# Decay blocks of an SSD branch: a preset and an accumulating transfer in place of a subtraction on VectorE

## The chip, the cores and the metric

The kernel runs on one core of one Trainium2 chip. The metric is the device time of one execution in microseconds (us), median of three runs. Lower is better.

## The reference, cut to what matters

The program is a decoder trunk of two layers on 256 tokens of width 1024. A layer is half a SwiGLU feed-forward (FFN), a token mixer, and another half FFN. The mixer runs two branches on one normalised input: a gated DeltaNet branch and a Mamba-2 state-space (SSD) branch, and merges them. The change lies in the SSD branch, which works in two chunks of 128 tokens with 32 heads in 4 groups of 8:

```python
a_cum = jnp.cumsum(log_a, axis=2)
seg = a_cum[:, :, :, None] - a_cum[:, :, None, :]
decay = jnp.where(causal, jnp.exp(jnp.where(causal, seg, 0.0)), 0.0)
cb = jnp.einsum("bclgn,bcsgn->bclsg", Cc, Bc)
y_diag = jnp.einsum("bclsg,bclsgh,bcsghp->bclghp", cb, decay, xdt)
```

For each group, chunk and head the kernel needs the 128 by 128 block cb times exp(a_cum[l] - a_cum[s]), zero where l is before s.

## The kernel before, in words

TensorE does all large products in three passes of split operands: a weight tile wraw (128 x 1024) comes in by a transfer from SP's queue, ScalarE rounds it to a high part whi, VectorE forms the low part wlo = wraw - whi, and TensorE multiplies. There are five buffers each for wraw, whi and wlo (`NRAW`, `NSPL`), so weights are prepared up to five tiles ahead. These two splits are the bulk of the work of ScalarE and VectorE throughout.

Inside a mixer the work is a list of named steps, `ORDER`. The tail of it is what concerns us: `... R R P R g100 g101 D0 S0 x10 T0 D1 x11 g110 g111 S1 x20 T1 o x21 N D2 y S2 D3 x30 x31 T2 ...`. R is a step of the DeltaNet recurrence; P forms the masked products cb of the SSD branch; g are gate products; x10 and x11 are the two units that make the inputs xs of group 1; D*g* makes the decay block of group *g*, S*g* and T*g* are the two halves of its SSD step; o and N are the branch product of DeltaNet, y the first transposes for that of the SSD branch. The list gives a priority. The framework's scheduler then sets the order in which instructions stand on each engine, and at run time each engine works strictly in that order; an instruction that waits holds all behind it on its engine.

Names that the text uses, with their lines:

- dc (L1060): the decay block of a group, 128 x 2048 floats, partition s, and along the row head, chunk and l. It lives in slot sA for groups 0 and 2 and sB for 1 and 3; those slots belong to kP and qP of the recurrence until the products ksb and qsb (L954) of its last step have read them, and dc2 takes dc0's slot once ydb (L1115) has read it, dc3 that of dc1.
- In `decay` (L1059): a transfer from SP's queue (L1061) broadcasts eight rows of a_cum, written to DRAM earlier (rdram), to all 128 partitions; VectorE subtracts the partition's own a_cum (ac), broadcast along the row; VectorE clamps at 0 from above (L1071, recorded as L78); ScalarE takes the exponential (L1072, recorded as L68); VectorE multiplies with the masked cb, cbm (L1073, recorded as L71).
- cbb (L1045, L1046): the four products of P, in PSUM banks of a rotating set of four. The fourth needs the bank that vb <- ob, os (L998), the last output of the recurrence, reads on VectorE. cbt holds the masked products.
- `ssd(g)` (L1087): xsb transposes of xsT, VectorE forms xD, xdt and xe, TensorE multiplies ydb = dc x xdt and yob, VectorE adds up into yz, ScalarE squares it (jk), the sums are sss, GpSimd takes the power -0.5 (srr, L210), ScalarE scales yz with it.
- `conv` (L625): ca on ScalarE, three steps on VectorE (ca, L74), then xsT by a SiLU on ScalarE. The exponential and the SiLU need different function tables, so an ACT_TABLE_LOAD stands between them.
- `dn_T` (L1150): transposes oT, og on VectorE, its high part bh on ScalarE, its low part bl on VectorE; these are the stationary operands of the branch product b (L335 to L337). `ss_T` makes the transposes yT for the SSD branch.

Two helpers record most lines: every ScalarE operation has L68, every two-operand VectorE operation L71. GpSimd otherwise does small powers and the accumulating transfers of the FFN (wsum at L156, h at L460).

Of the kernel before, what the change touches and what calls it, by code (L numbers as in the profile page):

```python
# [10 lines left out]
AF = mybir.ActivationFunctionType  # L11
ALU = mybir.AluOpType
# [4 lines left out]
P = 128  # L17
# [36 lines left out]
def trunk_kernel(ctx, tc, x, wst, wsm, norms, lpar, rpar, cst, out):  # L54
    nc = tc.nc
    V, A, G, PE = nc.vector, nc.scalar, nc.gpsimd, nc.tensor
# [10 lines left out]
    def act(o, i, func=AF.Copy, **kw):  # L67
        return A.activation(out=o, in_=i, func=func, **kw)  # L68

    def tt(o, a, b, op):  # L70
        return V.tensor_tensor(out=o, in0=a, in1=b, op=op)  # L71
# [4 lines left out]
    def ts(o, a, s1, op0, sc2=None, op1=None):  # L76
        if op1 is None:
            return V.tensor_scalar(out=o, in0=a, scalar1=s1, scalar2=None, op0=op0)  # L78
        return V.tensor_scalar(out=o, in0=a, scalar1=s1, scalar2=sc2, op0=op0, op1=op1)
# [7 lines left out]
    def trb(name):  # L87
        return trp.tile([P, 512], F32, tag="tr", name=name)
# [4 lines left out]
    def small(shape, name, bufs=2):  # L93
        return sm.tile(shape, F32, tag=name, name=name, bufs=bufs)
# [124 lines left out]
    h = cpool.tile([P, 2, D], F32, name="h")  # L219
# [373 lines left out]
    def mixer(l, nxt):  # L593
# [51 lines left out]
        ac = small([P, 2, 40], "ac", 1)  # L645
# [3 lines left out]
        rdram = dram.tile([40, S], F32, tag="rdram", name="rdram")  # L649
# [376 lines left out]
        late = {}  # L1026
# [11 lines left out]
        def ssd_pre():  # L1038
            BT, CT = late["BC"][:, 0:4], late["BC"][:, 4:8]
            cbt = slots.tile([P, 3 * GS, P], F32, tag="sF", name="cbt")  # L1040
            late["cbx"] = cbx = cbt[:, 2 * GS :]
            late["cbm"] = cbm = cbt[:, : 2 * GS].rearrange("p (g t) l -> p g t l", g=GS)
            for g in range(GS):
                cbb = trb("cbb")
                PE.matmul(cbb[:, 0 : 2 * P], BT[:, g, 0:P], CT[:, g, :], start=True, stop=True)  # L1045
                PE.matmul(cbb[:, 2 * P : 3 * P], BT[:, g, P : 2 * P], CT[:, g, P : 2 * P], start=True, stop=True)  # L1046
                tt(
                    cbm[:, g],
                    cbb[:].rearrange("p (t o l) -> p t o l", t=2, o=2)[:, :, 0, :],
                    U[:, None, :].to_broadcast([P, 2, P]),  # L1050
                    ALU.mult,
                )
                act(cbx[:, g], cbb[:, P : 2 * P])
            yield

        xsT = {}
# [1 line left out]

        def decay(g):  # L1059
            dc = slots.tile([P, 8, 2, P], F32, tag=("sA", "sB")[g % 2], name="dc")  # L1060
            nc.sync.dma_start(  # L1061
                dc[:].rearrange("p h t l -> p (h t l)"),
                rdram[8 * g : 8 * g + 8].rearrange("a b -> (a b)").partition_broadcast(P),
            )
            tt(
                dc[:], dc[:],
                ac[:, :, 8 * g : 8 * g + 8].rearrange("p t h -> p h t")[:, :, :, None].to_broadcast([P, 8, 2, P]),
                ALU.subtract,
            )
            dv = dc[:].rearrange("p h t l -> p (h t l)")  # L1070
            ts(dv, dv, 0.0, ALU.min)  # L1071
            act(dv, dv, AF.Exp)  # L1072
            tt(dc[:], dc[:], late["cbm"][:, g, None].to_broadcast([P, 8, 2, P]), ALU.mult)  # L1073
            decs[g] = dc

# [133 lines left out]
        def step(name):  # L1209
# [10 lines left out]
            elif kind == "M":  # L1220
                masks()
            elif kind == "I":
                next(inv, None)
            elif kind == "R":
                next(rc, None)
            elif kind == "b":
                bcm(*num)
            elif kind == "d":
                zdm(*num)
            elif kind == "x":  # L1230
                xs_unit(*num)
            elif kind == "P":
                drain(ssd_pre())
            elif kind == "D":
                decay(*num)
            elif kind == "g":
                gate(*num)
            elif kind == "S":
                heads[num[0]] = ssd(*num)
                next(heads[num[0]])  # L1240
            elif kind == "T":
                drain(heads[num[0]])
            elif kind == "o":
                dn_T(0)
            elif kind == "y":
                ss_T(0)
            elif kind == "N":
                dn_branch()
# [190 lines left out]
```

## Time and profile before

| | us |
|---|---|
| median of three runs (1543.25 to 1544.58) | 1544.3 |
| span of the profiled execution, first to last instruction | 1539.7 |
| between the two | 4.6 |
| TensorE busy | 1522.8 |
| VectorE busy | 1229.7 |
| ScalarE busy | 944.8 |
| GpSimd busy | 81.8 |

The granted clock is 0.999. Engines: PE is TensorE's matmuls and PEld its weight loads, DVE is VectorE, ACT is ScalarE, POOL is GpSimd, SP is the queue of most transfers. A row of a timeline reads: start, duration, engine, line, operation, output <- inputs, shapes, and in brackets how long the engine stood idle before and who ended that. A row of waits reads: who waited, for whom, us in total, times, the longest. A row of a tile has the shortest, median and longest duration in ns. A row of DMA queues has packets, MB, and the share of all sixteen DMA engines over the span. Times count from the start of the span; layer 0's mixer makes its decay blocks between 394 and 495, layer 1's 761 us later.

### The profile page before, as it was taken

What the parts mean: (1) busy time and instruction counts of PE and PEld (TensorE: products, weight loads), DVE (VectorE), ACT (ScalarE), POOL (GpSimd) and SP (SyncE); (2) the same over time, 40 slices, a digit from 0 to 9 for tenths busy, and PEclk for the clock granted to TensorE, in tenths of its full rate; (3) what the DMA queues carried; (4) which work ended last, traced back from release to release, by engine and by line L of the source; (5) the groups of instructions that cost most, each with busy time, mean ns of one, the idle gap of its engine ahead of it and who ended that gap; (6) DMA issues with size and microseconds to landing.
All of it is one profiled execution on the core that took longest, in us unless ns stands there. A gap on an engine that the chain in (4) does not pass through costs nothing.

```text
span 1539.7 us, 29072 instructions
## 1 busy us (share of the span) xinstructions
PE 1522.8 (99%) x11473; PEld 1384.4 (90%) x11473; DVE 1229.7 (80%) x1859; ACT 944.8 (61%) x1532; POOL 81.8 (5%) x92
## 2 busy tenths in 40 slices
PE   8999999999999999999999999999999999999998
PEld 7999889999888888999899998899998888899997
DVE  6878769967899766789778887689589996677886
ACT  5655667765665645555555566676756666455565
POOL 0000110000000000000100012010000000000010
PEclk9999999999999999999999999999999999999999
DMA  7687775653565556587867687665345555556785
GB/s 277 190 265 231 226 228 167 187 164 111 178 213 171 163 166 196 185 256 211 261 225 225 208 253 229 197 193 180 117 141 202 179 170 186 176 177 195 247 241 156
DMA packets 98831, 305.73 MB, mean 199 GB/s; under 512 B 22837, under 2 KB 23813, under 8 KB 97670
## 3 DMA queue, kind: packets, MB, share of 16 engines
q1 hardware_dynamic: 93796, 290.95, 57.2%
q0 software_dynamic: 4608, 12.58, 5.1%
q8 instruction: 90, 1.47, 0.4%
q14 instruction: 47, 0.39, 0.1%
q10 hardware_dynamic: 290, 0.33, 0.1%
HBM read 297.72 MB, written 1.92 MB: 195 GB/s over the span
## 4 chain that ended last, share of the span: by engine, by line
PE 89%; DVE 4%; ACT 2%; DMA 2%; issue 1%; SPq 1%; POOL 0%; POOLq 0%; ACTq 0%; DVEq 0%
PE fc L346 10%; PE fc L340 9%; PE fc L345 9%; PE t L366 9%; PE o L337 4%; PE o L335 4%; PE o L336 4%; PE f L366 3%; PE b L335 3%; PE b L337 3%; PE b L336 3%; PE p L336 2%; PE p L337 2%; PE p L335 2%; PE xs L345 1%; PE xs L340 1%
## 5 line engine op out<-in xcount | busy, mean ns | idle before, releaser
L71 DVE TENSOR_TENSOR wlo<-wraw,whi 128x1024 fp32r<-128x1024 f32 x488 | 591.8, 1221 | 186.7 <-ACT whi L68 172.2
L68 ACT ACTIVATE whi<-wraw 128x1024 fp32r<-128x1024 f32 x488 | 511.6, 1059 | 271.0 <-PE fc L345 92.5
L346 PE MATMUL fc<-uW,wlo 128*128 128x256 f32 x1280 | 354.9, 277 | 0.0
L340 PE MATMUL fc<-uW,whi 128*128 128x256 f32 x1280 | 354.1, 277 | 0.0
L345 PE MATMUL fc<-uW,whi 128*128 128x256 f32 x1260 | 348.3, 276 | 0.0
L340 PEld LDWEIGHTS fc<-uW,whi 128*128 128x128 f32 x1280 | 240.5, 188 | 0.8
L346 PEld LDWEIGHTS fc<-uW,wlo 128*128 128x128 f32 x1280 | 240.5, 188 | 0.0
L345 PEld LDWEIGHTS fc<-uW,whi 128*128 128x128 f32 x1260 | 236.5, 188 | 0.8
L366 PE MATMUL t<-whi,uW 128*128 128x512 f32 x512 | 165.3, 397 | 0.0
L366 PEld LDWEIGHTS t<-whi,uW 128*128 128x128 f32 x512 | 95.9, 188 | 21.6 <-issue 1.3
L68 ACT ACTIVATE whi<-wsum 128x1024 fp32r<-128x1024 f32 x64 | 68.0, 1062 | 58.8 <-PE fc L345 32.9
L366 PE MATMUL t<-wlo,uW 128*128 128x512 f32 x256 | 100.2, 392 | 0.0
L71 DVE TENSOR_TENSOR wlo<-wsum,whi 128x1024 fp32r<-128x1024 f32 x64 | 78.2, 1221 | 7.9 <-ACT whi L68 5.6
L335 PE MATMUL b<-whi,bh 128*128 128x512 f32 x192 | 76.1, 398 | 0.3
L336 PE MATMUL b<-wlo,bh 128*128 128x512 f32 x192 | 74.9, 390 | 0.0
L337 PE MATMUL b<-whi,bl 128*128 128x512 f32 x192 | 74.2, 393 | 0.0
L340 PE MATMUL xs<-uW,whi 128*128 128x256 f32 x256 | 72.8, 284 | 0.0
L346 PE MATMUL xs<-uW,wlo 128*128 128x256 f32 x256 | 71.4, 279 | 0.0
L345 PE MATMUL xs<-uW,whi 128*128 128x256 f32 x254 | 70.6, 278 | 0.0
L335 PE MATMUL o<-whi,gh 128*128 128x512 f32 (+1 forms) x160 | 62.0, 388 | 0.0
L337 PE MATMUL o<-whi,gl 128*128 128x512 f32 (+1 forms) x160 | 61.8, 386 | 0.0
L336 PE MATMUL o<-wlo,gh 128*128 128x512 f32 (+1 forms) x160 | 61.7, 386 | 0.0
(337 smaller groups left out, 3291.7 us busy)
## 6 DMA issues: line engine op xcount, KB each, us to landing
wraw<-in_wst_dram SPq DMA_DIRECT2D x504, 512.0 KB, 4.9
wsum<-in_wst_dram SPq DMA_DIRECT2D x16, 512.0 KB, 7.3
wsum<-in_wst_dram POOLq DMA_DIRECT2D x16, 512.0 KB, 8.7
dc<-rdram SPq DMA_DIRECT2D x8, 1024.0 KB, 8.5
nw<-in_norms_dram SPq DMA_DIRECT2D x6, 512.0 KB, 5.9
h<-u POOLq DMA_DIRECT2D x12, 256.0 KB, 6.8
gb<-rdram SPq DMA_DIRECT2D x8, 256.0 KB, 5.6
h<-in_x_dram SPq DMA_DIRECT2D x4, 256.0 KB, 3.7
```

What stands on the lines that cost most here:

```text
L68: return A.activation(out=o, in_=i, func=func, **kw)
L71: return V.tensor_tensor(out=o, in0=a, in1=b, op=op)
L335: PE.matmul(ps, lh, rh, start=start, stop=False)
L336: PE.matmul(ps, lh, rl, start=False, stop=False)
L337: return PE.matmul(ps, ll, rh, start=False, stop=stop)
L340: PE.matmul(ps, wh, mh, start=start, stop=False)
L345: PE.matmul(ps, wh, ml, start=False, stop=False)
L346: PE.matmul(ps, wl, mh, start=False, stop=stop)
L366: ins = PE.matmul(ps[t][:], st, mv, start=k0 == 0 and j == 0, stop=k0 == KT - 2 and j == 5)
```

## The change

ScalarE first writes the negated row term into the block, -ac broadcast along the row; then GpSimd issues a transfer that adds the broadcast rows of rdram to what stands there; VectorE's subtraction is gone. Clamp, exponential and multiply stay. The exponential is queued on ScalarE behind the last read of cbb (`issue_after` sets an order on that instruction's own engine alone, so it does not hold the clamp on VectorE).

```diff
-                act(cbx[:, g], cbb[:, P : 2 * P])
+                late["read"] = act(cbx[:, g], cbb[:, P : 2 * P])
...
         def decay(g):
             dc = slots.tile([P, 8, 2, P], F32, tag=("sA", "sB")[g % 2], name="dc")
-            nc.sync.dma_start(
-                dc[:].rearrange("p h t l -> p (h t l)"),
-                rdram[8 * g : 8 * g + 8].rearrange("a b -> (a b)").partition_broadcast(P),
+            dv = dc[:].rearrange("p h t l -> p (h t l)")
+            act(
+                dc[:],
+                ac[:, :, 8 * g : 8 * g + 8].rearrange("p t h -> p h t")[:, :, :, None].to_broadcast([P, 8, 2, P]),
+                scale=-1.0,
             )
-            tt(
-                dc[:], dc[:],
-                ac[:, :, 8 * g : 8 * g + 8].rearrange("p t h -> p h t")[:, :, :, None].to_broadcast([P, 8, 2, P]),
-                ALU.subtract,
+            G.dma_start(
+                out=dv, in_=rdram[8 * g : 8 * g + 8].rearrange("a b -> (a b)").partition_broadcast(P), accum_op=ALU.add
             )
-            dv = dc[:].rearrange("p h t l -> p (h t l)")
-            ts(dv, dv, 0.0, ALU.min)
-            act(dv, dv, AF.Exp)
+            with tc.issue_after(late["read"].ins):
+                ts(dv, dv, 0.0, ALU.min)
+                act(dv, dv, AF.Exp)
             tt(dc[:], dc[:], late["cbm"][:, g, None].to_broadcast([P, 8, 2, P]), ALU.mult)
```

The scheduler answers with another order at several places; both layers get the same. On VectorE, at the end of the recurrence in layer 0, before:

```order
L71 TENSOR_TENSOR wlo<-wraw,whi 128x1024 x2
L71 TENSOR_TENSOR dc<-dc,ac 128x2048
L71 TENSOR_TENSOR vb<-ob,os 128x512
L71 TENSOR_TENSOR cbt<-cbb,cs 128x256 x2
L1004 TENSOR_REDUCE so<-o_4924 128x4
L71 TENSOR_TENSOR cbt<-cbb,cs 128x256
L74 SCALAR_TENSOR_TENSOR so<-so,oe 128x4
L71 TENSOR_TENSOR cbt<-cbb,cs 128x256
L71 TENSOR_TENSOR vb<-vb,so_2294 128x512
L78 TENSOR_SCALAR dc<-dc 128x2048
L71 TENSOR_TENSOR dc<-dc,ac 128x2048
```

At the same place now (so is the recurrence's sum of squares, the two dc are blocks 0 and 1):

```order
L71 TENSOR_TENSOR wlo<-wraw,whi 128x1024
L78 TENSOR_SCALAR dc<-dc 128x2048
L71 TENSOR_TENSOR vb<-ob,os 128x512
L71 TENSOR_TENSOR cbt<-cbb,cs 128x256 x2
L1004 TENSOR_REDUCE so<-o_4924 128x4
L71 TENSOR_TENSOR cbt<-cbb,cs 128x256
L74 SCALAR_TENSOR_TENSOR so<-so,oe 128x4
L71 TENSOR_TENSOR cbt<-cbb,cs 128x256
L71 TENSOR_TENSOR vb<-vb,so_2294 128x512
L78 TENSOR_SCALAR dc<-dc 128x2048
L71 TENSOR_TENSOR dc<-dc,cbt 128x2048
```

The clamp of block 0, which waits for its transfer, now stands where the subtraction stood, ahead of vb; the clamp of block 1 stands where the second subtraction stood. The multiply of block 1 has moved ahead of xD, xdt and xe of group 0, from behind the products ydb.

On ScalarE, between the two squares of group 0 and the last convolution of x11, before (the exponential of block 2 comes further down, behind the next unit's ca):

```order
L68 ACTIVATE jk,sss<-yz 128x512 x2
L68 ACTIVATE whi<-wraw 128x1024
L68 ACTIVATE ca<-xs,lp 128x256
L68 ACTIVATE yz<-yz,srr 128x512 x2
L68 ACTIVATE whi<-wraw 128x1024
L68 ACTIVATE xsT<-ca 128x256
L68 ACTIVATE whi<-wraw 128x1024 x2
L68 ACTIVATE xsT<-ca 128x256
L68 ACTIVATE ca<-xs,lp 128x256
```

The same place now:

```order
L68 ACTIVATE jk,sss<-yz 128x512
L68 ACTIVATE ca<-xs,lp 128x256
L68 ACTIVATE whi<-wraw 128x1024
L68 ACTIVATE xsT<-ca 128x256
L68 ACTIVATE yz<-yz,srr 128x512 x2
L68 ACTIVATE whi<-wraw 128x1024
L68 ACT_TABLE_LOAD
L68 ACTIVATE dc<-dc 128x2048
L68 ACT_TABLE_LOAD
L68 ACTIVATE xsT<-ca 128x256
L68 ACTIVATE ca<-xs,lp 128x256
```

The exponential of block 2, with a table load on each side, has moved up to directly behind the scaling of yz and ahead of the last convolution. On VectorE the clamp and the multiply of block 2 have moved up with it, ahead of that convolution's three steps, and sss of group 0 has moved back behind two weight splits.

On ScalarE, at the start of the branch product of DeltaNet, before:

```order
L68 ACTIVATE jk,sss<-yz 128x512
L68 ACTIVATE ca<-xs,lp 128x256
L68 ACTIVATE bh<-og 128x512
L68 ACTIVATE xsT<-ca 128x256
L68 ACTIVATE yz<-yz,srr 128x512 x2
```

The same place now (yz and srr are those of group 1, bh the first two operands of b):

```order
L68 ACTIVATE xsT<-ca 128x256
L68 ACTIVATE jk,sss<-yz 128x512
L68 ACTIVATE ca<-xs,lp 128x256
L68 ACTIVATE whi<-wraw 128x1024
L68 ACTIVATE yz<-yz,srr 128x512 x2
L68 ACTIVATE bh<-og 128x512 x2
```

The first bh has moved from ahead of the scaling of yz to behind it. On TensorE two transposes oT and the four transposes of the first yT have moved ahead of the first b; on GpSimd the four transfers stand between the powers so and srr.

## The prediction

> **What bounds the kernel now.** I read the page first, then the waits of TensorE, then the time windows of the mixer of layer 0 (the 400:480 stretch; layer 1 repeats it 761 us later).
>
> ```profile
> span 1539.7 us, 29072 instructions
> ...
> PE 1522.8 (99%) x11473; PEld 1384.4 (90%) x11473; DVE 1229.7 (80%) x1859; ACT 944.8 (61%) x1532; POOL 81.8 (5%) x92
> ...
> PE 89%; DVE 4%; ACT 2%; DMA 2%; issue 1%; SPq 1%; POOL 0%; POOLq 0%; ACTq 0%; DVEq 0%
> ```
>
> TensorE is busy for 99% of the span and holds 89% of the chain that ended last. Taking work off another engine pays only where TensorE stands still, and any new stop of TensorE is a loss at full size. So the next view is who makes TensorE wait, and where the other engines are nearly full:
>
> ```profile
> PE cbb L1045 <- DVE vb L71: 1.9, 2, 1.3
> PE xsb L1101 <- ACT xsT L68: 1.9, 2, 0.9
> ...
> 400.00:420.00 20.00, 19.40 (x114) 16.61 (x113) 18.40 (x20) 12.27 (x16) 1.01 (x1) 1.00 0.48 172
> 420.00:440.00 20.00, 20.00 (x174) 17.56 (x173) 19.40 (x29) 13.26 (x22) 1.61 (x1) 1.00 0.68 221
> 440.00:460.00 20.00, 18.92 (x193) 17.43 (x192) 19.90 (x29) 14.50 (x20) 1.34 (x1) 1.00 0.64 210
> ```
>
> In a window the third busy figure, after PE and PEld, is VectorE: 18.4 to 19.9 of 20 us, so it really is full where the decay blocks are made. Yet TensorE loses only 1.9 us at cbb and 1.9 us at xsb, both layers together. That sum, 3.8 us, is the most that relief of VectorE can give here: 0.25% of the time.
>
> **The change part by part.** The operations on a decay block, eight in all (four per layer, dc0 to dc3 below):
>
> ```profile
> L1061 SPq DMA_DIRECT2D dc<-rdram x8: 326/404/1490, 394.0 to 1212.5; - x8
> L71 DVE TENSOR_TENSOR dc<-dc,ac x8: 2277/2284/2292, 401.9 to 1231.4; 128x2048 f32<-128x2048 f32 x8
> L78 DVE TENSOR_SCALAR dc<-dc x8: 1216/1220/1224, 408.3 to 1248.8; 128x2048 f32<-128x2048 f32 x8
> L68 ACT ACTIVATE dc<-dc x8: 1903/1918/1924, 411.0 to 1252.3; 128x2048 f32<-128x2048 f32 x8
> ...
> DMA to landing us min/median/max: 6.2/8.5/10.6
> ```
>
> Removed: 8 subtractions of 2.28 us on VectorE, 18.3 us, of which at most the 3.8 us above can show. Added: 8 presets on ScalarE. Before has no such operation; the nearest row is the exponential of the same 128x2048 shape, 1.9 us, and I take that. 15 us more on ScalarE, itself 12 to 15 us busy in 20, are covered, except where the order puts a preset ahead of something TensorE needs. The plain transfer leaves SP's queue (its weight loads move up, worth nothing as TensorE never waits for them there) and becomes an accumulating one on GpSimd, issued only after the preset. What that one costs:
>
> ```profile
> q1 hardware_dynamic: 93796, 290.95, 57.2%
> q0 software_dynamic: 4608, 12.58, 5.1%
> ...
> wsum<-in_wst_dram POOLq DMA_DIRECT2D x16, 512.0 KB, 8.7
> ...
> L156 POOL DMA_DIRECT2D wsum<-in_wst_dram x16: 862/870/1035, 69.6 to 1485.8; - x16
> ```
>
> q0 carries the accumulating transfers. By bytes, q1 takes 57.2% / 290.95 MB x 1539.7 us = 3.0 us of all sixteen engines per MB, q0 5.1% / 12.58 x 1539.7 = 6.2 us. A block is 1.05 MB: 3.2 us plain, 6.5 us accumulating. So from issue to landing I expect the quickest plain block plus the difference, 6.2 + 3.3 = 9.5 us, as the low estimate, and the median accumulating 512 KB plus another half, 8.7 + 3.3 = 12.0, as the high one. I take 9.5: the DMA share of the 400:420 window is 0.48, the lowest of the three. Issuing holds GpSimd 0.9 us, and GpSimd is otherwise idle.
>
> The Trainium skill, DMA: Bandwidth & Descriptors, section "Anatomy of one DMA — SWDGE (gpsimd) path", fits a transfer issued from GpSimd as about 2.0 us plus its bytes at 436 GB/s; by that a block lands 4.4 us after issue, an estimate, and the first term below would be -1.9 and not +1.8. The trace does not agree for accumulating transfers: half a block takes 8.7 us.
>
> *First place: cbb, after dc0.* VectorE's order keeps vb directly behind the first operation on dc0, formerly the subtraction, now the clamp, so whoever waits for dc0 holds vb, and vb holds TensorE's fourth cbb. (GpSimd's power for so also stands behind two block issues, which are long over by then.)
>
> ```profile
> 391.29 1.09 PE L954 MATMUL ksb<-St,kP 128*64 128x128 f32 x16
> ...
> 392.25 0.55 ACT L68 ACTIVATE ca<-xs,lp 128x256 f32<-128x256 f32 x1
> ...
> 404.15 0.68 DVE L71 TENSOR_TENSOR vb<-ob,os 128x512 f32<-128x512 f32 x1
> ...
> 408.34 1.22 DVE L78 TENSOR_SCALAR dc<-dc 128x2048 f32<-128x2048 f32 x1
> ...
> 404.88 0.48 PE L1045 MATMUL cbb<-BC 128*128 128x256 f32 x1 [0.60 <-DVE vb L71]
> ...
> 1152.94 0.55 ACT L68 ACTIVATE ca<-xs,lp 128x256 f32<-128x256 f32 x1
> ...
> 1166.25 0.48 PE L1045 MATMUL cbb<-BC 128*128 128x256 f32 x1 [1.28 <-DVE vb L71]
> ```
>
> dc0's slot is free when ksb ends at 392.4; ScalarE is free at 392.8. Preset to 394.7, landing at 404.2, clamp 1.2 to 405.4, vb 0.7 to 406.1; cbb then starts 1.3 us later than its 404.88. In layer 1 the same steps from 1153.5 give 1155.4, 1164.9, 1166.8: 0.5 us later than 1166.25. Together +1.8. Were the landing at 6.2, both old waits would vanish (0.6 and 1.28: -1.9); at 12.0 it is +6.8.
>
> *dc1* follows in the same queue: 404.2 + 6.5 = 410.7 at the earliest, some 413 with weight loads between. VectorE comes to its clamp 3.5 us after vb's end (the old 404.8 to 408.34), at 409.6, and stops for 1 to 3.5 us, where the second subtraction stood with 2.3. Queued behind are dc0's multiply, weight splits and the inputs of ydb; five weight buffers cover the splits. I take 0.3 us per layer, bounds 0 and 3: +0.6.
>
> *Second place: xsb.* On ScalarE the exponential of dc2 now stands behind the scaling of yz, which waits for GpSimd's srr; and on VectorE dc2's multiply stands ahead of the last convolution of the xs unit, whose result (xsT) the last transposes of xsb need.
>
> ```profile
> 426.81 1.28 ACT L68 ACT_TABLE_LOAD   x1 [3.56 <-DVE ca L74]
> ...
> 431.29 1.61 POOL L210 TENSOR_TENSOR srr<-sss,mhalf 128x2 f32<-128x2 f32 x1 [23.59 <-DVE sss L79]
> ...
> 432.93 1.34 ACT L68 ACTIVATE yz<-yz,srr 128x512 f32<-128x512 f32 x2 [1.32 <-POOL srr L210]
> ...
> 443.56 0.47 DVE L74 SCALAR_TENSOR_TENSOR ca<-xs,lp,ca 128x253 f32<-128x253 f32 x1
> 444.12 0.42 ACT L68 ACTIVATE xsT<-ca 128x256 f32<-128x256 f32 x1 [1.26 <-DVE ca L74]
> ...
> 444.59 0.33 PE L1101 MATMUL xsb<-cs,xsT 128*128 128x128 f32 x1 [0.93 <-ACT xsT L68]
> ...
> L71 DVE TENSOR_TENSOR wlo<-wraw,whi 128x1024 fp32r<-128x1024 f32 x488 | 591.8, 1221 | 186.7 <-ACT whi L68 172.2
> L68 ACT ACTIVATE whi<-wraw 128x1024 fp32r<-128x1024 f32 x488 | 511.6, 1059 | 271.0 <-PE fc L345 92.5
> ```
>
> srr started at 431.29. Ahead of it now stand two weight splits (2.4) and three convolution steps (1.4) more, a multiply (2.3) less: +1.5, and TensorE's 1.6 us of lateness, so 434.4. Then srr 1.6, yz 1.3, whi 1.1, table 1.3, exponential 1.9, multiply 2.3, three steps 1.4, a split 1.2, xsT 0.4: 446.9. TensorE, late by 1.6, would come there at 444.59 - 0.93 + 1.6 = 445.3. It waits 1.6 us, or 2.7 where dc1's multiply, moved ahead of ydb's inputs, costs VectorE half its length; I take 2.4, which is 1.5 more than the old 0.93. Two layers: +3.0, bounds -1.9 (the wait goes, as the subtraction does) and +5.
>
> *Third place: the first b.* bh, which the branch product b needs, stood ahead of the scaling of yz on ScalarE; now it stands behind it.
>
> ```profile
> 458.41 0.17 DVE L79 TENSOR_SCALAR sss<-sss 128x2 f32<-128x2 f32 x1
> ...
> 458.66 1.61 POOL L210 TENSOR_TENSOR srr<-sss,mhalf 128x2 f32<-128x2 f32 x1 [25.77 <-DVE sss L79]
> ...
> 458.76 0.62 ACT L68 ACTIVATE bh<-og 128x512 fp32r<-128x512 f32 x1
> ...
> 460.30 1.34 ACT L68 ACTIVATE yz<-yz,srr 128x512 f32<-128x512 f32 x2 [0.61 <-POOL srr L210]
> ...
> 451.09 0.33 SPq L1061 DMA_DIRECT2D dc<-rdram  x1
> ...
> 458.58 0.71 PE L1154 MATMUL oT<-cs,vb 128*128 128x128 f32 x5
> 459.44 0.50 PE L335 MATMUL b<-whi,bh 128*128 128x512 f32 x1
> ```
>
> With sss as early as before, yz ends at 461.6, bh at 462.2, and b starts there instead of at 459.44. Six transposes (0.14 each) move into that gap, 0.8 us, so 2.0 us is lost; sss itself comes some 0.3 later, as a step of xsT moved ahead of its square. 2.3 per layer: +4.6, bounds +1.5 and +8 for both layers. dc3's slot came free at 451.1, when SP issued the plain transfer; a preset later, 453.0, the new one is issued and lands at 462.5. VectorE comes to that clamp behind the bl that follows bh, after 462.2, so I cost it at nothing, and at 2.5 us per layer if the landing takes 12.0.
>
> Sum: 1.8 + 0.6 + 3.0 + 4.6 = +10.0 us on a span of 1539.7; the median of 1544.3 lies 4.6 above the span, and I leave that offset: 1554.3.
>
> **The rivals.** *The accumulating transfer is quick and the full VectorE decides.* Blocks land in about 6 us, VectorE is rid of 18.3 us in its fullest stretches, and the waits at cbb and xsb go: -3.8 us, and with bh's inputs ready no new one: 1540.5. For it: VectorE at 19.9 of 20. Against: q0's price per byte, and b's new place behind yz does not depend on the transfer. It decides where a block lands in under 8.6 us, from which cbb is no later than before (it is late by 0.9 us a layer at 9.5), and sss comes 2 us earlier, so that bh is ready when b is. Chance 0.07. The Trainium skill's fit above is this case.
>
> *Waits are exchanged.* cbb comes out even, the xsb gaps close (-1.9) because VectorE is lighter, b costs less than 1.5 a layer: 1542 to 1546. The gaps were made on VectorE, and a lighter one could bring sss early enough. Chance 0.20.
>
> *GpSimd cannot issue while VectorE works.* The Trainium skill, SBUF — State Buffer, section "Who interferes with whom", says a transfer issued by GpSimd starves while VectorE is in a two-port mode. The mechanism here: each of the first three issues per layer slips behind clamps and splits on a VectorE that is never idle, by one such operation, 1.2 us, and dc1's late landing reaches ydb: another 3.6 to 5 us per layer: 1561 to 1564. Sixteen issues of 862 to 1035 ns on a VectorE 80% busy speak against it: spread 0.17 us. Chance 0.13.
>
> That the change does not do what it says can be left out: the order has the presets and transfers and no subtraction.
>
> **How the numbers follow.** The forecast, the new places of exponential and bh cost more than the relief brings, +4 to +16 us, has 0.60. About 0.2%, 3.1 us, is what a measurement of this kernel can tell from no change. Slower by more: 0.60 + 0.13 = 0.73; within: 0.20; faster: 0.07. The range 1544 to 1564 leaves out the faster rival, half of the exchange case and a few hundredths above.
>
> **What would show it.** In the changed profile: presets near 1.9 us; accumulating blocks landing after 9 us or more; VectorE's wait before the first clamp ended by the DMA; TensorE's cbb wait near 2 us, its xsb wait near 2.4, and a new wait at the first b, near 2, released by ScalarE's bh. If b shows no wait, or landings are at 6 us, the steps that carry the forecast are wrong.

## The result and the profile after

The changed kernel takes 1556.7 us (median of five runs, 1553.8 to 1557.0), the kernel before 1544.0 (five runs, 1543.2 to 1544.6): a ratio of 1.0083, 95% interval 1.0072 to 1.0094, 12.7 us slower. The profiled execution was the quickest of its five, 1553.8, with a span of 1552.0, 12.3 more than the 1539.7 of before.

The page of the changed kernel, its span, busy times, the queue of GpSimd's transfers and the chain that ended last:

```profile
span 1552.0 us, 29084 instructions
...
PE 1524.9 (98%) x11473; PEld 1386.5 (89%) x11473; DVE 1213.9 (78%) x1851; ACT 959.0 (62%) x1540; POOL 87.6 (6%) x100
...
q0 software_dynamic: 5760, 20.97, 7.9%
...
PE 79%; DVE 6%; issue 6%; ACT 4%; DMA 3%; SPq 1%; POOL 1%; POOLq 0%; ACTq 0%; DVEq 0%
```

VectorE is 15.8 us less busy, and TensorE's share of the chain fell from 89% to 79%: it now waits. For whom, the waits of TensorE say:

```profile
PE cbb L1045 <- DVE vb L71: 6.3, 2, 3.3
PE b L335 <- ACT bh L68: 5.2, 2, 2.6
...
PE xsb L1101 <- ACT xsT L68: 1.9, 3, 1.0
```

Against before, cbb rose from 1.9 to 6.3, a wait at the first b is new, and xsb has the same sum. The rows of the decay blocks (shortest, median, longest in ns) and their landing:

```profile
L68 ACT ACTIVATE dc<-ac x8: 1901/1914/1935, 393.8 to 1222.6; 128x2048 f32<-128x2048 f32 x8
L1067 POOL DMA_DIRECT2D dc<-rdram x8: 867/912/931, 396.0 to 1224.8; - x8
...
  DMA dc<-rdram: 14.1, 6
...
DMA to landing us min/median/max: 9.3/10.6/14.1
```

A preset takes 1.9 us, a block lands 10.6 us after issue (8.5 before), and six of the eight clamps had to wait for that, 14.1 us in all. The two places in layer 0, VectorE's rows first, then TensorE's, ScalarE's, and TensorE's again:

```profile
406.81 1.23 DVE L78 TENSOR_SCALAR dc<-dc 128x2048 f32<-128x2048 f32 x1 [3.76 <-DMA dc<-rdram]
407.95 0.68 DVE L71 TENSOR_TENSOR vb<-ob,os 128x512 f32<-128x512 f32 x1
```

```profile
408.69 0.70 PE L1045 MATMUL cbb<-BC 128*128 128x256 f32 x2 [3.33 <-DVE vb L71]
```

```profile
465.81 1.33 ACT L68 ACTIVATE yz<-yz,srr 128x512 f32<-128x512 f32 x2 [0.54 <-POOL srr L210]
467.05 0.61 ACT L68 ACTIVATE bh<-og 128x512 fp32r<-128x512 f32 x1
```

```profile
467.71 0.50 PE L335 MATMUL b<-whi,bh 128*128 128x512 f32 x1 [2.59 <-ACT bh L68]
```

Both are as the order has them: VectorE stands 3.76 us before the clamp with vb behind it; bh stands behind yz's scaling. A third loss shows in the windows just after that last stop (the third figure from the right is the granted clock, then come DMA share and GB/s):

```profile
466.00:468.00 2.00, 0.28 (x1) 0.29 (x2) 1.03 (x2) 1.66 (x3) 0.00 (x0) 1.00 0.99 354
468.00:470.00 2.00, 2.00 (x7) 1.55 (x7) 2.00 (x5) 0.53 (x1) 0.00 (x0) 0.66 0.97 373
470.00:472.00 2.00, 2.00 (x6) 1.51 (x6) 2.00 (x4) 1.98 (x4) 0.00 (x0) 0.50 0.26 104
472.00:474.00 2.00, 2.00 (x10) 1.64 (x9) 1.41 (x3) 1.99 (x2) 0.00 (x0) 0.99 0.00 0
```

TensorE comes back from its stop busy, but from 468.6 to 472.0 it is granted half its clock: 7 and 6 products in 2 us instead of 10. That costs 1.7 us more, which no wait shows.

Where the 12.3 us of the spans went, from how much later than in before TensorE starts the same step: 1.1 before the mixer of layer 0 (the row wait of the start-up alone is 0.8 longer), 8.1 in that mixer, 3.3 in layer 1's, and −0.3 between. The 1.1 is no part of the change: over the fourteen profiled executions of this document the mixer of layer 0 starts 0.8 us earlier to 1.6 later than in before, and 1.5 later in a kernel with the operations of before and its order up to there (the one with one instruction moved, below).

### The profile page after: what moved, and what is told of

It is laid out like the page before. It is cut to its first block, busy times and chain, and to the rows that moved or that the text cites. A ratio compares the mean times of both kernels' runs of the same rounds, so it can differ in the third digit from the quotient of the medians.

```text
span 1552.0 us, 29084 instructions
## 1 busy us (share of the span) xinstructions
PE 1524.9 (98%) x11473; PEld 1386.5 (89%) x11473; DVE 1213.9 (78%) x1851; ACT 959.0 (62%) x1540; POOL 87.6 (6%) x100
## 4 chain that ended last, share of the span: by engine, by line
PE 79%; DVE 6%; issue 6%; ACT 4%; DMA 3%; SPq 1%; POOL 1%; POOLq 0%; ACTq 0%; DVEq 0%
PE fc L346 9%; PE fc L340 9%; PE fc L345 9%; PE t L366 9%; PE o L337 4%; PE o L336 4%; PE o L335 4%; PE f L366 3%; PE b L335 3%; PE b L337 3%; PE b L336 3%; DMA dc<-rdram 2%; DVE ca L74 2%; PE p L336 2%; PE p L337 2%
## 6 DMA issues: line engine op xcount, KB each, us to landing
dc<-rdram POOLq DMA_DIRECT2D x8, 1024.0 KB, 10.6
```

## The experiments

The theory was that of the two places: an instruction that waits for something late stands ahead of one that TensorE needs. The rivals: the slow transfer costs by itself, wherever it lands; or ScalarE's presets do; or the order costs and the operations don't.

A scheduler that is asked to move one instruction moves others too. So, except for the two plain transfers, each kernel has the place of every instruction on its engine written out, and each is queued behind the one ahead of it (issue order alone, no wait). An experiment then differs from the kernel that it starts from in the rows named with it. No run fixes a kernel in its own order without any other change; but the kernel before with one instruction moved is fixed in this way too, and up to that instruction it keeps step with before to 0.1 us in every stretch of the mixer.

```diff
     with tile.TileContext(nc) as tc:
         trunk_kernel(tc, *args)
+        pin(tc)
...
+def pin(tc):
+    traced = {i.name: i for i in tc.nc.cur_bb.bb.instructions}
+    for line in PLACE:
...
+        for a, b in zip(names, names[1:]):
+            info = mybir.DependencyInfo(mybir.DependencyClass.NoSync, mybir.DependencyReason.DATA)
+            tc.add_manual_dep(traced[b], a, info, reason="pin")
```

**The two places, each by itself and together.** Block 0's clamp on VectorE, both layers alike:

```diff
-L78 TENSOR_SCALAR dc<-dc 128x2048
 L71 TENSOR_TENSOR vb<-ob,os 128x512
 L71 TENSOR_TENSOR cbt<-cbb,cs 128x256 x2
...
 L71 TENSOR_TENSOR vb<-vb,so_2294 128x512
-L78 TENSOR_SCALAR dc<-dc 128x2048
+L78 TENSOR_SCALAR dc<-dc 128x2048 x2
```

> The changed kernel with every instruction at its place on its engine, but for the clamp of block 0, which stands on VectorE directly ahead of the clamp of block 1, behind vb and the four cbt products. Transfer, preset and everything else are untouched. Theory of the two places (the loss is made where an instruction that waits for something late stands ahead of one that TensorE needs: 6.3 us at cbb, 5.2 us at the first b): the cbb wait of 6.3 us goes, the wait at b stays, some 1550.5 us, 6.5 over the kernel before. Rival, the slow transfer costs by itself (it lands 10.6 us after issue, and its traffic holds up weights; the stop moves on to ydb, which needs block 0): no gain, 1555 to 1557. Rival, ScalarE's eight presets make the loss: no gain either, 1555 to 1557.

1551.2 us, ratio to before 1.0053 (1.0040 to 1.0066). The cbb wait is gone; TensorE's waits, and VectorE's row at the second clamp:

```profile
PE b L335 <- ACT bh L68: 5.3, 2, 2.6
PE xsb L1101 <- ACT xsT L68: 3.0, 3, 1.0
...
PE ydb L1115 <- DVE xdt L71: 2.2, 2, 1.3
```

```profile
412.93 1.23 DVE L78 TENSOR_SCALAR dc<-dc 128x2048 f32<-128x2048 f32 x1 [4.00 <-DMA dc<-rdram]
```

As expected in time, but not all of the 6.3 us came back: VectorE now stands 4.0 us before the clamp of block 1, and ydb and xsb wait 3.3 more for what is queued behind it.

The first bh on ScalarE:

```diff
+L68 ACTIVATE bh<-og 128x512
 L68 ACTIVATE yz<-yz,srr 128x512 x2
-L68 ACTIVATE bh<-og 128x512 x2
+L68 ACTIVATE bh<-og 128x512
```

> The changed kernel with every instruction at its place, but for the first bh of each layer, which stands on ScalarE ahead of the two scalings of yz of group 1. Theory of the two places: the wait of 5.2 us at the first b goes down to under 0.5, the cbb wait of 6.3 stays, some 1551.5 us. Rivals (the transfer by itself, or ScalarE's load): TensorE then waits at that place for something else, bl or weights, and the time stays at 1555 to 1557.

1551.4 us, 1.0054 (1.0043 to 1.0065): the time is as expected, while the wait at the first b is 1.5 us and not under 0.5. TensorE's waits:

```profile
PE cbb L1045 <- DVE vb L71: 6.2, 2, 3.2
...
PE b L335 <- ACT bh L68: 1.5, 2, 0.8
```

Both moves together (the two diffs above):

> Both moves at once: block 0's clamp behind vb and cbt, the first bh ahead of yz's scaling. Theory of the two places: the waits of 6.3 and 5.2 us both go, and 1545 to 1547 us are left; what stands above the 1542 that before would have without its own 1.9 us at cbb is the step at xsb. Were the places even the whole of it and VectorE's 18 us of relief worth something, it would be under 1542. Rivals (the transfer, or ScalarE): over 1552.

1548.0 us, 1.0035 (1.0023 to 1.0047): the two places are worth 0.48%, 7.4 of the 12.7 us, and the time is 1 us over the expected range. What is left is the late block 1, and smaller waits at b:

```profile
PE ydb L1115 <- DVE xdt L71: 2.5, 2, 1.5
...
PE xsb L1101 <- ACT xsT L68: 2.2, 3, 1.0
PE b L337 <- DVE bl L71: 1.6, 3, 0.9
PE b L335 <- ACT bh L68: 1.5, 2, 0.8
```

**What the accumulation costs.** The order of the changed kernel on every engine is unchanged without any pins; only the addition goes, or the queue too. Both leave the row term out of the decay.

```diff
-            G.dma_start(
-                out=dv, in_=rdram[8 * g : 8 * g + 8].rearrange("a b -> (a b)").partition_broadcast(P), accum_op=ALU.add
-            )
+            G.dma_start(
+                out=dv, in_=rdram[8 * g : 8 * g + 8].rearrange("a b -> (a b)").partition_broadcast(P)
+            )
```

> The changed kernel, order on every engine the same, but GpSimd's transfer writes the column term over the preset and does not add: the row term is left out of the decay. It prices the accumulation alone. If accumulating makes the transfer slow, blocks land some 3 us earlier, in 6 to 8 us instead of 10.6; by the theory of the two places the cbb wait goes from 6.3 to 0 to 2.5 us and the wait at b, which no transfer enters, stays at about 5: 1551 to 1553 us. If a transfer from GpSimd is slow whether it adds or not, landings stay at 9 to 11 us and the time at 1555 to 1557. If the transfer's slowness is the whole loss: 1543 to 1546.

1545.7 us, 1.0021 (1.0012 to 1.0030). The expectation of 1551 to 1553 failed, and the rival's 1543 to 1546 held. The issues, landings and waits of TensorE:

```profile
L1067 POOL DMA_DIRECT2D dc<-rdram x8: 538/582/642, 394.5 to 1214.1; - x8
...
DMA to landing us min/median/max: 6.8/7.4/7.6
```

```profile
PE b L335 <- ACT bh L68: 5.3, 2, 2.6
...
PE xsb L1101 <- ACT xsT L68: 0.5, 2, 0.3
```

Landing falls from 10.6 to 7.4 us and the cbb wait vanishes, as expected, and the wait at b is still 5.3. What the expectation left out is that xsb's wait goes to 0.5 as well, since VectorE has no subtraction and hardly waits for blocks, that cbb starts 0.4 and 1.4 us earlier than before, and that the transposes moved ahead of b are missing behind it: −4.5 us in all against b's +5.9.

```diff
-            G.dma_start(
-                out=dv, in_=rdram[8 * g : 8 * g + 8].rearrange("a b -> (a b)").partition_broadcast(P), accum_op=ALU.add
-            )
+            nc.sync.dma_start(
+                out=dv, in_=rdram[8 * g : 8 * g + 8].rearrange("a b -> (a b)").partition_broadcast(P)
+            )
```

> The changed kernel with the same order on VectorE, ScalarE and TensorE, but the transfer is a plain one from SP's queue that overwrites the preset (the row term is left out of the decay), so GpSimd issues none. It tells the queue from the accumulation: with GpSimd's plain transfer the time was 3.1 us over before. If GpSimd's queue or its issues cost nothing, this is within 2 us of that, 1544 to 1548; if SP's weight loads hold the block up, landings reach 9 us and the cbb wait comes back: 1548 to 1553.

1545.9 us, 1.0015 (1.0005 to 1.0026), as expected where the queue costs nothing:

```profile
DMA to landing us min/median/max: 6.9/7.1/7.5
```

So GpSimd's queue is not what is slow; the addition is.

**Order and operations, crossed.** First the operations of before in the changed kernel's order:

```diff
+L71 TENSOR_TENSOR dc<-dc,ac 128x2048
 L78 TENSOR_SCALAR dc<-dc 128x2048
...
-L68 ACTIVATE dc<-ac 128x2048
...
-L1067 DMA dc<-rdram 128x2048 x2
```

> The operations of the kernel before (plain transfer from SP's queue, subtraction on VectorE, no preset) in the order of the changed kernel on every engine: each subtraction stands directly ahead of its clamp, the first bh behind yz's scaling. It prices the order without the new operations. If the order makes the loss, the wait at the first b is there with some 5 us, and cbb starts a clamp (1.2 us) later per layer than before: 2.4 more; with VectorE no lighter, 1551 to 1554 us. If the accumulating transfer makes it, as the plain transfer in that order (3.1 us over before) suggests for most of it, only the 3 us of b are left: 1546 to 1548. If both are needed, 1544 to 1546.

1555.4 us, 1.0076 (1.0064 to 1.0089): with not one of the new operations, the order costs nearly as much as the change did. The waits:

```profile
PE b L335 <- ACT bh L68: 5.2, 2, 2.6
PE cbb L1045 <- DVE vb L71: 4.0, 2, 2.4
```

The time is over the upper end of the expectation, 1554, which had nothing for the clock: half speed followed three of this kernel's stops in the profile (2.45, 2.62 and 2.62 us long) and took 6.8 us. But at cbb the two kernels lose in different ways. Here the block's transfer is nearly in time, and VectorE does the subtraction and the clamp, 3.5 us of work, ahead of vb; in the changed kernel it stands waiting for the transfer.

```profile
403.68 2.29 DVE L71 TENSOR_TENSOR dc<-dc,ac 128x2048 f32<-128x2048 f32 x1 [0.97 <-DMA dc<-rdram]
406.00 1.23 DVE L78 TENSOR_SCALAR dc<-dc 128x2048 f32<-128x2048 f32 x1
```

With the two plain transfers above, which have no subtraction and land early, the same order cost 0.21% and 0.15%. So the order's price depends on what stands in it.

Then the new operations in the order of before:

```diff
-L71 TENSOR_TENSOR dc<-dc,ac 128x2048
 L71 TENSOR_TENSOR vb<-ob,os 128x512
...
+L68 ACTIVATE dc<-ac 128x2048
 L68 ACTIVATE os<-qsb,eG 128x128 x4
+L68 ACTIVATE dc<-ac 128x2048
```

> The changed kernel's operations (preset, accumulating transfer from GpSimd, no subtraction) in the order of the kernel before on every engine: block 0's clamp behind vb and cbt, bh ahead of yz's scaling, the exponential and the multiply of block 2 late; the presets and issues stand where the changed kernel has them. It prices the operations without the order. The cbb wait is gone (1.9 us less than before); block 0 still lands late and ydb waits for its product, some 1 us per layer; nothing else moves: 1542.5 to 1546 us by the theory that the loss takes an order that leans on an early landing. If the slow transfer or the presets cost wherever they stand: 1548 or more.

1548.4 us, 1.0032 (1.0020 to 1.0045): the theory's range ended at 1546, the rival with "wherever they stand" began at 1548. Not the transfer, though, for which VectorE and ScalarE waited once, for 0.2 us:

```profile
  DMA dc<-rdram: 0.2, 1
```

TensorE waits at ob (1.3 and 1.1 us, for vn, behind two presets on ScalarE) and again at the first b. The wait at ob, then ScalarE's rows at the first b in layer 0, and TensorE's:

```profile
PE ob L995 <- ACT vn L68: 2.3, 2, 1.3
```

```profile
451.36 1.91 ACT L68 ACTIVATE dc<-ac 128x2048 f32<-128x2048 f32 x1 [0.63 <-PE ydb L1115]
453.29 1.28 ACT L68 ACT_TABLE_LOAD   x1
454.58 1.92 ACT L68 ACTIVATE dc<-dc 128x2048 f32<-128x2048 f32 x1
...
461.20 0.62 ACT L68 ACTIVATE bh<-og 128x512 fp32r<-128x512 f32 x1
```

```profile
461.88 0.80 PE L335 MATMUL b<-whi,bh 128*128 128x512 f32 x1 [2.33 <-ACT bh L68]
```

Block 3's preset waits 0.63 us for its slot and takes 1.91, and bh starts 2.4 us later than in before (461.20 against 458.76), with TensorE itself 0.3 late by then. So a preset costs nothing as busy time of ScalarE, and about its full length where it stands ahead of what TensorE needs.

**One instruction.** The kernel before, with only the first bh moved:

```diff
-L68 ACTIVATE bh<-og 128x512
 L68 ACTIVATE xsT<-ca 128x256
 L68 ACTIVATE yz<-yz,srr 128x512 x2
+L68 ACTIVATE bh<-og 128x512
```

> The kernel before, operations and order, but for one instruction per layer: the first bh stands on ScalarE behind yz's scaling and not ahead of it. It is the place at the first b by itself. From the kernel before: yz ended at 461.6, so bh ends at 462.2 and b starts some 2.8 us later, per layer: 5.6 us. If half speed of the clock follows such a stop (10 of the 19 stops of 2.3 us or more so far were followed by a granted clock of 0.5 for 3.4 or 6.8 us, costing 1.7 or 3.4), there are 0 to 7 us more: some 1549 to 1553. If bh's place costs only where the accumulating transfer or the presets are there too, the time stays at 1543 to 1545.

1552.9 us, 1.0061 (1.0046 to 1.0077). One 0.6 us instruction, moved past three others, costs 0.61%, 9.4 us. TensorE's waits, and the windows around the stop in layer 0:

```profile
PE b L335 <- ACT bh L68: 5.8, 2, 2.9
```

```profile
462.00:464.00 2.00, 0.14 (x1) 0.14 (x1) 0.16 (x1) 2.00 (x4) 0.00 (x0) 0.83 0.74 217
464.00:466.00 2.00, 2.00 (x5) 1.62 (x6) 2.00 (x5) 1.14 (x2) 0.00 (x0) 0.50 0.11 45
466.00:468.00 2.00, 2.00 (x9) 1.52 (x9) 2.00 (x3) 0.66 (x3) 0.00 (x0) 0.82 0.00 0
```

TensorE starts b 2.8 us late per layer, as expected. The rest is the clock: 1.7 us behind each stop here, and over the five timed runs a mean granted clock of 0.9964 against 0.9990 of before, 0.26% or 4.0 us.

**Is there an order in which the operations pay?** First whether a win at cbb is kept without them, by the subtraction of block 0 in the kernel before:

```diff
-L71 TENSOR_TENSOR dc<-dc,ac 128x2048
 L71 TENSOR_TENSOR vb<-ob,os 128x512
...
 L71 TENSOR_TENSOR vb<-vb,so_2294 128x512
+L71 TENSOR_TENSOR dc<-dc,ac 128x2048
 L78 TENSOR_SCALAR dc<-dc 128x2048
```

> The kernel before with every instruction at its place but for the first subtraction of each layer, which stands on VectorE behind vb and the four cbt products, directly ahead of its own clamp. If a stop at cbb costs its full size, the 1.9 us there go and the time is 0.8 to 2 us under before, 1541 to 1543; if the subtraction is then late for ydb, block 0's product comes 2.3 us later and the gain is given back there: 1543 to 1545.

1544.8 us, 1.0010 (1.0002 to 1.0019). Not kept: cbb's wait is gone, and xsb's is up from 1.9.

```profile
PE xsb L1101 <- ACT xsT L68: 4.7, 2, 2.4
```

The expectation had the loss at ydb; it came at xsb, behind the block products on VectorE. By the table below the exchange is nearly even, −2.1 us at cbb and +2.8 at xsb; the mean granted clock of the timed runs, 0.9981 against 0.9990, is worth 1.4 us by itself, nearly the whole 1.5 that the ratio says.

Now the new operations in the order of before, with the presets where nothing waits behind them:

```diff
 L68 ACTIVATE vn<-vnb 128x512
+L68 ACTIVATE dc<-ac 128x2048
 L68 ACTIVATE o_4924<-vb 128x512
...
 L68 ACTIVATE bh<-og 128x512
 L68 ACTIVATE xsT<-ca 128x256
+L68 ACTIVATE dc<-ac 128x2048
...
 L71 TENSOR_TENSOR xe<-xdt,dE 128x512
+L78 TENSOR_SCALAR dc<-dc 128x2048
```

> The changed kernel's operations in the order of before, with the presets out of the way: block 1's preset behind vn on ScalarE, block 3's behind the xsT that follows the second bh (its issue behind srr of group 1 on GpSimd), block 1's clamp behind xe and its exponential three weight splits later. If the presets' places on ScalarE made what was left with the old order (1.1 to 1.3 us at ob, 2.3 at b, per layer, and a clock at half speed behind it), these go, and the waits at cbb and xsb are gone too: some 3 to 4.5 us under before, 1539 to 1541. If the accumulating transfers cost by themselves: 1545 or more. If VectorE's relief is worth nothing: 1543 to 1544.

1545.2 us, 1.0012 (1.0003 to 1.0021), not the expected 1539 to 1541 but the 1545 of the rival in which the transfers cost by themselves. Up to the first b it was ahead of before by 1.5 us in layer 0 and 2.6 in layer 1, as expected; then it lost 3.6 and 3.7. ScalarE's row there:

```profile
480.37 1.06 ACT L68 ACTIVATE whi<-wraw 128x1024 fp32r<-128x1024 f32 x1 [5.17 <-DMA wraw<-in_wst_dram]
```

A weight tile is late while block 3's transfer, issued at 470.2, runs. So block 3's preset goes directly behind the first bh:

```diff
 L68 ACTIVATE bh<-og 128x512
+L68 ACTIVATE dc<-ac 128x2048
 L68 ACTIVATE xsT<-ca 128x256
 L68 ACTIVATE yz<-yz,srr 128x512 x2
...
-L68 ACTIVATE dc<-ac 128x2048
```

> As the tuned order, but the preset of block 3 stands on ScalarE directly behind the first bh, so that its transfer is issued near 459.5 and not at 470. The tuned order won 1.5 us in layer 0 and 2.5 in layer 1 up to the first b and lost 3.6 and 3.7 us behind it, where ScalarE waited 5.2 us for a weight tile while block 3's accumulating transfer ran. If that transfer's traffic in the stretch that is short of weights made the loss, the gain is kept: 1538.5 to 1541 us. If the 1.2 us by which yz and the second bh come later make a new stop at b, 1542 to 1545. If block 3's place had nothing to do with it: 1545 again.

1540.9 us, 0.9988 (0.9979 to 0.9997): quicker than before, if by little. The weight tile waits 1.25 us instead of 5.17, and of cbb and xsb TensorE's waits show nothing any more:

```profile
475.69 1.06 ACT L68 ACTIVATE whi<-wraw 128x1024 fp32r<-128x1024 f32 x1 [1.25 <-DMA wraw<-in_wst_dram]
```

What it still loses behind the first b, 1.2 and 1.1 us, it loses for the most part at short waits for the next bh and bl (0.4 and 0.6 us, both layers together).

Last, the operations of before in that order (block 0's subtraction and clamp behind cbt, block 1's behind xe):

```diff
-L71 TENSOR_TENSOR dc<-dc,ac 128x2048
 L71 TENSOR_TENSOR wlo<-wraw,whi 128x1024
-L78 TENSOR_SCALAR dc<-dc 128x2048
...
 L71 TENSOR_TENSOR xe<-xdt,dE 128x512
+L71 TENSOR_TENSOR dc<-dc,ac 128x2048
+L78 TENSOR_SCALAR dc<-dc 128x2048
```

> The operations of the kernel before (plain transfer, subtraction on VectorE) in the order of the version that was 0.12% faster than before, as far as the operations are there: block 0's subtraction and clamp behind vb and cbt, block 1's behind xe, its exponential three weight splits later. It tells whether that version's gain comes from the order alone or needs the operations. If VectorE's relief by the subtractions is what keeps the win at cbb from being given back at xsb, xsb waits 2.4 us per layer as in the kernel with only the first subtraction moved, and the time is 1543 to 1546; if the order alone does it: 1540 to 1542.

1549.7 us, 1.0041 (1.0027 to 1.0055), above the expected 1543 to 1546: the wait at xsb is 3.3 us, not 2.4, and half speed follows it, 1.7 us in each layer.

```profile
PE xsb L1101 <- ACT xsT L68: 7.6, 4, 3.3
```

So the quicker version needs the new operations: in its order they are worth 0.53%, 8.2 us; in the order that the scheduler made (1.0083 against 1.0076), nothing.

**All runs in one table.** How much later than in before TensorE gets through each stretch of the mixer, layer 0 / layer 1, in us, worked out from the timelines of the profiled executions (up to the first xsb; to the first ydb; to the second group's ydb; to the first b; to the end of the branches), and the mean granted clock of the timed runs (before: 0.9987 to 0.9992); the intervals of the ratios stand above. What half speed cost is counted in the stretch in which it fell, 3.4 of the 4.8 us of bh early for one:

| kernel | cbb | ydb | xsb | b | behind b | clock | ratio |
|---|---|---|---|---|---|---|---|
| changed kernel | 2.9/1.9 | 0.2/0.0 | 0.9/−0.8 | 3.1/3.0 | 1.0/−0.7 | 0.9964 | 1.0083 |
| clamp late | −0.7/−1.4 | 1.4/1.2 | 1.4/0.7 | 3.0/3.0 | 1.0/−0.7 | 0.9972 | 1.0053 |
| bh early | 2.7/4.8 | 0.0/0.0 | −0.7/−0.7 | 1.1/1.1 | 0.0/−0.1 | 0.9965 | 1.0054 |
| both | −0.7/−1.4 | 1.5/1.1 | 0.7/1.0 | 1.1/1.1 | 1.2/−0.1 | 0.9992 | 1.0035 |
| plain, GpSimd | −0.4/−1.4 | 0.0/0.2 | −0.7/−0.8 | 3.0/3.0 | −0.6/−0.8 | 0.9980 | 1.0021 |
| plain, SP | −0.7/−1.4 | 0.0/0.0 | −0.8/−0.7 | 2.9/2.9 | 0.9/0.6 | 0.9975 | 1.0015 |
| old operations, new order | 3.4/0.5 | 0.2/0.0 | −0.4/0.9 | 2.9/2.9 | 2.0/1.1 | 0.9960 | 1.0076 |
| new operations, old order | 0.4/−0.2 | 0.2/0.2 | −1.1/−1.1 | 2.2/2.2 | 1.9/2.0 | 0.9974 | 1.0032 |
| old, bh late | 0.1/0.1 | 0.0/0.0 | 0.0/0.0 | 2.8/2.8 | 1.5/1.6 | 0.9964 | 1.0061 |
| old, subtraction late | −0.7/−1.4 | 0.0/0.0 | 1.4/1.4 | 0.0/0.0 | 0.0/0.1 | 0.9981 | 1.0010 |
| tuned | −0.7/−1.5 | 0.0/0.0 | −0.8/−0.9 | 0.0/−0.2 | 3.6/3.7 | 0.9990 | 1.0012 |
| tuned, second | −0.7/−1.4 | 0.0/0.0 | −0.8/−0.8 | 0.0/0.0 | 1.2/1.1 | 0.9991 | 0.9988 |
| old, tuned order | −0.9/−1.5 | 0.0/0.0 | 4.6/4.6 | −0.2/−0.2 | 1.1/1.1 | 0.9968 | 1.0041 |

## Why the prediction was right or wrong

Slower by 12.7 us was measured and 10.0 predicted; the two places that carry the loss are the ones named, but the terms were less alike than their sum. That the sum came near is in part luck: the term for cbb was 3.0 us too small and the one for xsb 2.9 too large, and the clock, 4.0 us in the timed runs, stood in no term. The 4.6 us between span and time, which the forecast carried over, held as well (1556.7 less 1552.0 is 4.7), but for a reason that it did not have: in every timed run on record with its span the two lie about 1.8 us apart. By that the profiled execution of before took some 1541.5 us, an estimate, and was a quick one, as was that of the changed kernel.

*cbb, +1.8 predicted, +4.8 measured.* The mechanism is right: in the run with the clamp behind vb the wait went. The step that failed is the landing. The issue came when it was due (396.0, which is 394.7 and TensorE's 1.1 us of lateness), but the clamp of block 0 started 10.8 and 10.5 us after it in the two layers and not 9.5, 2.3 more together. Of the remaining 0.7, 0.5 is the product t that stood in front of the stop and now runs behind it.

*dc1, +0.6 predicted, 0.2 measured,* and for a reason the prediction did not give. Less the start-up's 1.1 us, block 1 landed at about 411.8, within the forecast's 410.7 to 413, but VectorE, held up before block 0, came to its clamp 1.5 us later than forecast and had 0.7 us left to wait in layer 0:

```profile
412.97 1.23 DVE L78 TENSOR_SCALAR dc<-dc 128x2048 f32<-128x2048 f32 x1 [0.71 <-DMA dc<-rdram]
```

With block 0's clamp out of the way the wait is there, 4.0 us on VectorE, and ydb is 1.4 and 1.2 late.

*xsb, +3.0 predicted, +0.1 measured.* Here the step "behind the scaling of yz, which waits for srr" named the wrong releaser. VectorE's clamp of block 2 and ScalarE's exponential in layer 0:

```profile
441.42 1.23 DVE L78 TENSOR_SCALAR dc<-dc 128x2048 f32<-128x2048 f32 x1 [3.60 <-DMA dc<-rdram]
```

```profile
442.68 1.92 ACT L68 ACTIVATE dc<-dc 128x2048 f32<-128x2048 f32 x1 [1.63 <-DVE dc L78]
```

The exponential waited for the clamp and the clamp for the transfer. Nor was the wait measured against the right arrival: TensorE came to xsb 3.1 us late from cbb in layer 0 and not 1.6, so that much less was left to wait, 1.6 us. In layer 1 only 0.3 was left, less than the old 0.9. So waits along one chain must not be added up as if each began on time.

*The first b, +4.6 predicted, about +4.5 measured:* +3.1 and +3.0, less the 0.7 to 0.8 us per layer of transposes that moved into the gap and are missing behind it. This step held in mechanism and size, and the kernel with only bh moved shows that it needs neither transfer nor preset.

*The clock was not in the prediction at all:* 1.7 us in the profiled execution; in the timed runs 0.9964 against 0.9990, 4.0 us of the 12.7.

*The rivals.* The quick transfer holds for a plain one at cbb and xsb, whose waits do go under the old ones, but not at b, where 5.3 us stay: 1545.7 us and not 1540.5. The Trainium skill's fit (DMA: Bandwidth & Descriptors, "Anatomy of one DMA — SWDGE (gpsimd) path"), 4.4 us for a block, agrees with neither row, both taken beside the weight loads: 7.4 us plain, 10.6 accumulating. GpSimd held up by VectorE can be ruled out here: the first issue stands 0.3 us behind the end of its preset, and all eight took 867 to 931 ns; the starving that the Trainium skill has in SBUF — State Buffer, section "Who interferes with whom", does not show. That is no test of the part of the rival that lies with the clamps, though: in the trace no clamp runs on VectorE beside any of the eight issues. The exchange of waits did not come: cbb lost 4.8 us and b over 2 in each layer, and the waits at xsb, which were to close, add up to 1.9 us as before.

What stays open is what decides whether half speed follows a given stop.

## What to carry to other kernels

An operation taken off a full engine is worth nothing until one knows where the scheduler puts what took its place: here the order that it made lost as much with the old operations as with the new, and the new operations in an order fitted by hand to their real landing times were 0.12% quicker than before. Look on each engine for the instruction that waits longest, and for what TensorE needs behind it. And price a stop of TensorE with the clock that may follow it, not by its own length.

## What the runs showed of the hardware

*A stop of TensorE can cost twice.* In the fourteen profiled executions TensorE stopped 23 times for 2.3 to 3.3 us (from the end of one product to the start of the next); behind 14 of these the granted clock was 0.50 for about 3.4 us (twelve times, 1.7 us lost) or 6.8 us (twice, 3.4 lost). Of the 38 stops of 1.0 to 2.1 us none had it. In the timed runs the three kernels without a long stop, both moves and the two tuned ones, have the clock of before, 0.9990 to 0.9992, and all that have one lie at 0.9960 to 0.9981. The Trainium skill, TensorE: Matmul & The Clock Gate, section "Part 1: The HAM clock gate", has a window of about 3.4 us that runs free and halves the clock after an idle one; the length of the slow stretches and that only some stops are hit agree, but half speed followed stops of 2.33 us here, well under its window and under the 3.4 us that the section "HAM oscillation — how this bites in real kernels" gives as the rule.

*An accumulating transfer takes the DMA engines twice as long as a plain one from the same queue.* Without GpSimd's other transfers (5.1% of 1539.7 us in before), the eight blocks took 7.9% of 1552.0 − 78.5 = 44 us of all sixteen engines accumulating, and 6.5% of 1541.3 − 78.5 = 22 us plain: 5.5 and 2.7 us a block. Issuing one takes 912 ns instead of 582.
